# Layer 2 of a two-layer recurrent trunk: keys and values turned by VectorE and through DRAM instead of by TensorE, Silu as one function, and another plan

## The chip, the cores and the metric

The kernel runs on one core of a Trainium2 chip. Its engines are TensorE (PE), VectorE (DVE), ScalarE (ACT), GpSimd (POOL) and SyncE (SP, which here only issues DMAs). The metric is the device time of one launch in microseconds, as the median of several runs.

## The reference

One step of a decoder trunk with two layers, over 1024 new prompt positions and 8 sampled sequences of 4 positions, 1056 tokens in all, with 1024 features. Layer 1 is an RG-LRU block. Layer 2, which the change is about, is an HGRN2 block with eight heads of 128 key and 128 value features:

```python
u = (rmsnorm(x) @ w_in)                    # 1024 -> 4 * 1024: q, f, iv, gate
q = silu(q)
log_g = logaddexp(log(lb), log1p(-lb) + log_sigmoid(f));  k = -expm1(log_g);  v = iv
# per head, a recurrence over time, computed in chunks:
#   S_t = exp(log_g_t) * S_(t-1) + k_t v_t^T ;  o_t = q_t S_t
o = o * rsqrt(mean(o * o) + EPS) * o_gain
x = x + (o * silu(gate)) @ w_out
```

Outputs are the final normed activations and the states of both layers.

## The kernel before, in words

Everything is stored with features on the 128 partitions and the 1056 tokens along the free dimension. Large products are made in three parts (`mm3`, L243 to L245): both operands are split into a high and a low part, and high times high, high times low and low times high are added in PSUM. The splits of weights are made by ACT (the high part, L380 and L1430) and POOL or DVE (the low part, L325).

**Order.** Each layer is written as a list of operations with costs, keys read and written, and priorities (class `Flow`). A planner on the host simulates the engines with these costs, turns the plan forward and back eight times, and issues all instructions in the order of the best plan. PE's operations marked `main` are chained, so their order is fixed by the program text. Layer 1 also runs a random search of 3000 tries over its first 60 us; layer 2 does not.

**Layer 2.** Heads 0 and 1 are projected with plain products (`item`, evacuation from L1001), heads 2 to 7 by `seven`: a scheme with seven half-size products in place of eight, called twice per head, first for queries and forget gates (`seven(h, 0, 1, ...)`), then for gates and values (`seven(h, 3, 2, ...)`). Four weight loads per call go out on SP (L1423). The finished quarters are settled in `settle`: forget gates by Tanh (L1511) and two affine steps (L1512, L1513), queries and gates by a hand-made Silu, `0.5 x (1 + tanh(0.5 x))` without its half: Tanh on ACT (L1517), then (t + 1) * x on DVE (L1518; in `item` L1018, in layer 1's `first1` L717). The missing halves are made good later: `4 * EPS` at L1299 and `hog`, half the output gain, at L1327.

**The recurrence.** Per head it is cut in chunks of 128 tokens, and within a chunk in levels 1, 2, 4 to 64: at each level DVE scales queries (row A) or keys (row B) by decays (`scale`, L1036, with ACT copying the other half, L1039), and PE makes small blocks of scores in column tiles (`diag`, L1054, and L1074, L1088, L1108, L1132, L1139). Four bursts per head are put between the big products. In their order:

- `burst1(h)`: levels 0 and 1 of head h. Of head h-1 the keys (both halves) and the second half of the values are turned by `transposed`: four PE transposes per half (L1163) into PSUM and an ACT copy to SBUF (L1169). The sampled tokens are turned apart (`samples`, L1175).
- `burst2(h)`: levels 2 and 4 of head h; of head h-1 the state products, `kt` times `vt` for each chunk (`states`, L1219, eight of 128 x 128 x 128), the sampled states (L1227) and their update (`advance`, L1248).
- `burst3(h)`: levels 8 and 16 of head h; outputs of head h-1 (`outs`, L1273 with the values, L1275 with the states), then Square sums on ACT (L1292) and the normalisation.
- `burst4(h)`: levels 32 and 64 of head h, and the first half of its values is turned; outputs of head h-1 are turned back and multiplied with the gate (`gated`, L1317, L1327).

The first two stand in the second call of `seven` for head h, the last two in the first call for head h+1.

So the keys of head h are final after `scale(h, 64, 0, 0)` in `burst4(h)` and are used in `burst2(h+1)`; the values are read there and in `burst3(h+1)`. Between `burst4(h)` and `burst2(h+1)` lie about eight pairs of big products. The turned keys `kt` share their buffer with the outputs `on`.

**After the heads** comes the output projection, whose first products (with the first five heads) cover the bursts of head 7, and the final norm.

Of the kernel before, what the change touches and what calls it, by code (L numbers as in the profile page):

```python
# [41 lines left out]
CH = 352  # L42
# [9 lines left out]
class Flow:  # L52
# [3 lines left out]
    HOP = 0.2  # L56
    ENGINES = ("PE", "DVE", "ACT", "POOL", "SP")
# [37 lines left out]
    def lag(self, i, j):  # L95
# [4 lines left out]
        return self.HOP + b[6] + (2.15 + a[5] / 250.0 if a[5] else 0.0)  # L100

    def plan(self, key, stop=None):
# [5 lines left out]
        free = dict.fromkeys(self.ENGINES, 0.0)  # L108
        dma = 0.0
# [4 lines left out]
        for _ in range(n):  # L114
# [6 lines left out]
            if both and free["POOL"] > t0:  # L121
                us = max(us, free["POOL"] - t0 + us - 0.13)
            starts[i] = t0
            free[e] = end = t0 + us
            if kb:
                dma = max(dma, t0 + 2.6) + kb / 250.0
                end = dma - 2.15 - kb / 250.0
            ends[i] = max(free[e], dma if kb else 0.0)
# [83 lines left out]
def tile_trunk(ctx: ExitStack, tc: tile.TileContext, xT, prm, hc, w0, wg, wo0, w1, wo1, s_in,  # L212
# [85 lines left out]
    with ExitStack() as l0:  # L298
# [15 lines left out]
        def act(n, emit, r, w, prio=5, more=0.0):  # L314
            fl.add("ACT", 0.25 + 0.0007 * n + more, emit, r, w, prio)

        def dve(n, emit, r, w, prio=5, both=False):
            fl.add("DVE", 0.13 + 0.0011 * n, emit, r, w, prio, both=both)

        def pool(n, emit, r, w, prio=5):  # L320
            fl.add("POOL", 0.1 + 0.00245 * n, emit, r, w, prio)
# [69 lines left out]
        def product(w, xs, step=8, more=()):  # L391
# [3 lines left out]
            for s in range(0, n, step):  # L395
# [6 lines left out]
                fl.add("PE", 0.48 * len(ks), emit, (*(q for k in ks for q in (*xs[k][2], *w(k)[2])), *more), (pk,), 1, main=True)  # L402
# [305 lines left out]
        def first1(i, c):  # L708
# [64 lines left out]
        def smalls1():  # L773
# [6 lines left out]
            nonlocal lc, lcn, lbc, hog  # L780
            mx, e0, e1, lb, lc, lcn, lbc, hog = (small(8) for _ in range(8))
# [14 lines left out]
            v(V.tensor_scalar, hog, pv("og"), 0.5, None, op0=ALU.mult)  # L796
# [41 lines left out]
        hbr = hbi = hbd = cn = cp = lc = lcn = lbc = hog = None  # L838
# [90 lines left out]
    with ExitStack() as l1:  # L929
        p1 = l1.enter_context(tc.tile_pool(name="l1", bufs=1, reuse_waits="tile"))  # L930
        fl = Flow(side=0.4)
# [21 lines left out]
        kt = fixed("kt", [128, 8, 128], F32, p1)  # L953
        on = kt
# [3 lines left out]
        vt = rows[5][:, :1024].rearrange("p (n d) -> p n d", n=8)  # L958
        SA = a_rows[1]
        for o, n, keys in ((at, 1024, ATK), (ad, 256, [("ad",)]), (as2, 64, [("as", 0), ("as", 1)]),  # L960
                           (ab, 288, [("ab",)])):
            pool(0.3 * n, lambda o=o: G.memset(o, 0.0), (), keys, 3)
# [852 lines left out]
```

## Time and profile before

| what | value |
|---|---|
| runs | 1060.86, 1060.86, 1060.49 us; median 1060.86 |
| profiled execution | span 1059.4 us from its first to its last instruction |
| between the span and the median of the runs | 1.5 us |
| instructions in the profile | 25677 |
| granted PE clock over the span | 0.996 |
| bytes moved by DMA | 103.07 MB, on average 97 GB/s |

The profile is that of one execution; the time of that execution itself, other than by its span, is not recorded, so its span is set beside the median. In its rows a number after L is a line of the kernel. PE lists its matmuls, PEld its weight loads. A float32 product leaves two matmul records, a transpose one. Durations of matmuls overlap, so neighbouring rows of the timeline are compared by their starts.

### The profile page before, as it was taken

The numbers are of one execution on the slowest core, as the hardware profiler recorded it, in microseconds if no ns is written. First come the engines' busy times: TensorE is split into PE (matmuls) and PEld (weight loads), VectorE is DVE, ScalarE is ACT, GpSimd is POOL, SyncE is SP. The second block draws the span as 40 slices with busy tenths as digits, with TensorE's granted clock in tenths as the row PEclk, the third lists the DMA queues.
The fourth block names the chain that finished last, engine by engine and source line by source line (L and its number), as shares of the span: only waits on it lengthen the run. The fifth ranks groups of instructions, "written<-read, shape, count | busy, mean of one in ns | idle before, by whom it ended". The sixth has DMA issues, their size and how long they took to land.

```text
span 1059.4 us, 25677 instructions
## 1 busy us (share of the span) xinstructions
PE 1050.1 (99%) x9964; PEld 1021.2 (96%) x9964; DVE 842.2 (79%) x1671; ACT 590.9 (56%) x1339; POOL 540.0 (51%) x601
## 2 busy tenths in 40 slices
PE   9999999999999999999999999999999999999997
PEld 9999999999999999999999999999999999999986
DVE  7999996888888689265799988988979797994536
ACT  6568656877775875233354474646464555652324
POOL 3425343444544366555667555555545565551544
PEclk9999999999999999999999999999999999999998
DMA  8201112123842595340211121212121221355204
GB/s 297 68 27 45 54 51 74 57 60 100 255 145 63 177 294 162 127 136 28 71 44 38 45 101 44 92 45 92 35 91 54 72 70 66 117 177 167 84 3 164
DMA packets 70121, 103.07 MB, mean 97 GB/s; under 512 B 9200, under 2 KB 50160, under 8 KB 70000
## 3 DMA queue, kind: packets, MB, share of 16 engines
q1 hardware_dynamic: 67696, 98.67, 29.2%
q10 hardware_dynamic: 2304, 2.77, 0.8%
q8 instruction: 78, 1.28, 0.5%
q14 instruction: 43, 0.35, 0.1%
HBM read 71.05 MB, written 25.49 MB: 91 GB/s over the span
## 4 chain that ended last, share of the span: by engine, by line
PE 89%; DVE 6%; DMA 2%; POOL 1%; issue 1%; ACT 0%; ACTq 0%; POOLq 0%; DVEq 0%; SPq 0%
PE mm L243 24%; PE mm L244 24%; PE mm L245 24%; PE hg L569 1%; PE hg L1054 1%; PE hg L1163 1%; DVE R L1370 1%; PE hg L1273 1%; DMA wraw<-in_w_dram 1%; PE hg L1219 1%; PE hg L243 1%; PE hg L244 1%; PE hg L245 1%; PE hg L1275 1%; DVE tmp L1370 1%
## 5 line engine op out<-in xcount | busy, mean ns | idle before, releaser
L243 PE MATMUL mm<-xh,whi 128*128 128x352 f32 (+1 forms) x1143 | 358.6, 314 | 0.0
L245 PE MATMUL mm<-xh,wlo 128*128 128x352 f32 (+1 forms) x1143 | 353.2, 309 | 0.0
L244 PE MATMUL mm<-xl,whi 128*128 128x352 f32 (+1 forms) x1143 | 353.1, 309 | 0.0
L325 POOL TENSOR_TENSOR wlo<-wraw,whi 128x256 fp32r<-128x256 f32 (+3 forms) x184 | 203.3, 1122 | 178.6 <-ACT whi L380 81.2
L244 PEld LDWEIGHTS mm<-xl,whi 128*128 128x128 f32 x1143 | 215.1, 188 | 1.5
L243 PEld LDWEIGHTS mm<-xh,whi 128*128 128x128 f32 x1143 | 214.7, 188 | 1.5
L245 PEld LDWEIGHTS mm<-xh,wlo 128*128 128x128 f32 x1143 | 214.8, 188 | 0.0
L501 DVE SCALAR_TENSOR_TENSOR k<-xb,prm_sb,k 128x352 f32<-128x352 f32 (+2 forms) x144 | 90.1, 637 | 10.9 <-ACT k L498 7.7
L243 PE MATMUL mm<-t,whi 128*128 128x264 f32 (+1 forms) x306 | 89.3, 292 | 0.0
L244 PE MATMUL mm<-t,whi 128*128 128x264 f32 (+1 forms) x306 | 87.7, 287 | 0.0
L245 PE MATMUL mm<-t,wlo 128*128 128x264 f32 (+1 forms) x306 | 87.4, 286 | 0.0
L1503 DVE TENSOR_TENSOR k<-mm,k 128x264 f32<-128x264 f32 x144 | 60.2, 426 | 20.5 <-PE mm L245 17.4
L325 POOL TENSOR_TENSOR wlo<-R,whi 128x256 fp32r<-128x256 f32 x64 | 60.1, 959 | 24.7 <-ACT whi L1430 24.7
L584 POOL TENSOR_TENSOR k<-X 128x352 f32<-128x352 f32 x36 | 44.9, 1257 | 47.8 <-DVE R L585 38.6
L380 ACT CAST whi<-wraw 128x512 fp32r<-128x512 f32 (+2 forms) x83 | 46.1, 574 | 30.1 <-PE mm L244 16.1
L243 PEld LDWEIGHTS mm<-t,whi 128*128 128x128 f32 x306 | 57.6, 188 | 0.2
L245 PEld LDWEIGHTS mm<-t,wlo 128*128 128x128 f32 x306 | 57.7, 188 | 0.0
L244 PEld LDWEIGHTS mm<-t,whi 128*128 128x128 f32 x306 | 57.6, 188 | 0.0
L1430 ACT CAST whi<-wraw 128x512 fp32r<-128x512 f32 x52 | 32.1, 618 | 36.3 <-PE mm L245 16.8
L243 PE MATMUL mm<-yh,whi 128*128 128x352 f32 x153 | 49.9, 326 | 0.0
L245 PE MATMUL mm<-yh,wlo 128*128 128x352 f32 x153 | 49.4, 323 | 0.0
L244 PE MATMUL mm<-yl,whi 128*128 128x352 f32 x153 | 49.4, 323 | 0.0
(481 smaller groups left out, 2634.3 us busy)
## 6 DMA issues: line engine op xcount, KB each, us to landing
wraw<-in_w_dram SPq DMA_DIRECT2D x90, 256.0 KB, 2.7
wraw<-in_wo_dram SPq DMA_DIRECT2D x34, 192.0 KB, 2.5
si<-in_s_in_dram SPq DMA_DIRECT2D x8, 512.0 KB, 3.8
out_ss_out_dram<-si SPq DMA_DIRECT2D x8, 512.0 KB, 2.6
R<-in_w_dram SPq DMA_DIRECT2D x15, 256.0 KB, 2.5
sg<-x1b SPq DMA_DIRECT2D x21, 176.0 KB, 2.9
x<-sg SPq DMA_DIRECT2D x21, 176.0 KB, 1.8
R<-td SPq DMA_DIRECT2D x72, 44.0 KB, 2.0
```

Of the source, the lines that this page charges most:

```text
L243: T.matmul(out, wh, xh, start=first, stop=False)
L244: T.matmul(out, wh, xl, start=False, stop=False)
L245: T.matmul(out, wl, xh, start=False, stop=last)
L325: emit = lambda: e.tensor_tensor(b, x, a.bitcast(F32), op=ALU.subtract)
L380: act(m, lambda hi=hi, raw=raw, m=m: S.copy(hi[:, :m], raw[:, :m]), rk, (hk,), prio)
L501: dve(u, lambda src=src, dst=dst, sh=sh, k=k: V.scalar_tensor_tensor(dst, sh(src, k), pc("cw", 12 * k + m), dst, op0=ALU.mult, op1=ALU.add ...
L569: fl.add("PE", 0.62, lambda ps=ps, i=i, c=c: T.matmul(ps[:96, :CH], gs[:, i, :], ST[:96, chunk(c)], start=True, stop=True), (("gs",), *((" ...
L584: pool(CH, lambda x=x, a=a, b=b: G.tensor_tensor(x, a.bitcast(F32), b.bitcast(F32), op=ALU.add), (ak, bk), (xk,), 3)
L1054: T.matmul(ps[32 * j:32 * j + 32, n * w:n * w + w], B[:, o:o + 32], q(slice(o, o + 32)), start=True, stop=True, tile_position=(0, 32 * j))
L1370: dve(n, lambda: V.tensor_tensor(o, a, b, op=op), r, (w,), prio, True)
L1430: act(512, lambda: S.copy(hi, raw), (rk,), (hk,), 2)
L1503: dve(QT, lambda: V.tensor_tensor(o[0], z[0], u[0], op=ALU.add), (z[1], u[1]), (o[1],), 0)
```

## The change

The change has three parts, all in layer 2 except for two lines of `first1`.

1. `transposed` goes. At the end of `burst4`, `turned` turns values and keys of the head: DVE transposes blocks of 32 x 32 over 1024 columns, the result is written to DRAM (512 KB) and read back in four parts of 128 KB, so that the 32-token blocks of each chunk land on their partitions. Afterwards the features of a row lie in four blocks of 32, 256 columns apart. A state product therefore becomes four, with 32 weight columns each, in four column tiles of PE; the values are read as a moving operand with four pieces.
2. Queries and gates get Silu on ACT in one step, straight from PSUM or the sums; the DVE step goes, and so do the factors that made up for the half.
3. The planner has its own costs for layer 2 (`exact`), starts from the time at which each engine ends layer 1, keeps SP's and ACT's DMA queues apart, and lets DVE operations marked `both` and POOL operations exclude each other. The search over the first 60 us is made for layer 2 too. The weight loads of `seven` go out on ACT's queue instead of SP's.

```diff
 class Flow:
+    HOPS = {"PE": 0.23, "DVE": 0.15, "ACT": 0.15, "POOL": 0.15, "SP": 0.2}
-    def __init__(self, until=None, side=1.2):
+    def __init__(self, until=None, side=1.2, busy=None):
+        self.busy = {e: (busy or {}).get(e, 0.0) for e in self.ENGINES}
+        self.exact = busy is not None
...
     def plan(self, key, stop=None):
-        free = dict.fromkeys(self.ENGINES, 0.0)
-        dma = 0.0
+        free = dict(self.busy)
+        locked = taken = 0.0
+        dma = {"SP": 0.0, "ACT": 0.0}
...
-            if both and free["POOL"] > t0:
+            if both and not self.exact and free["POOL"] > t0:
                 us = max(us, free["POOL"] - t0 + us - 0.13)
+            elif both and self.exact:
+                us += max(0.0, taken - t0 - 0.07)
+                locked = t0 + us
+            elif e == "POOL" and self.exact:
+                us += max(0.0, locked - t0 - 0.035)
+                taken = t0 + us
...
         def act(n, emit, r, w, prio=5, more=0.0):
-            fl.add("ACT", 0.25 + 0.0007 * n + more, emit, r, w, prio)
+            fl.add("ACT", (0.09 + 0.00088 * n if fl.exact else 0.25 + 0.0007 * n) + more, emit, r, w, prio)
...
         def first1(i, c):
-                act(CH, lambda: S.activation(o, ps[:, :CH], AF.Tanh, scale=0.5), (pk,), ok, 0)
-                dve(CH, lambda: V.scalar_tensor_tensor(o, o, 1.0, ps[:, :CH], op0=ALU.add, op1=ALU.mult), (pk, *ok), ok, 0)
+                act(CH, lambda: S.activation(o, ps[:, :CH], AF.Silu), (pk,), ok, 0)
...
-        fl = Flow(side=0.4)
+        last = {e: max(t[3] for t in fl.log if t[1] == e) for e in Flow.ENGINES}
+        fl = Flow(side=0.4, busy={e: max(0.0, t - last["PE"]) for e, t in last.items()})
...
-        vt = rows[5][:, :1024].rearrange("p (n d) -> p n d", n=8)
+        vflat = rows[5][:, :1024]
+        vt, kt = (o.rearrange("p (a n j) -> p n a j", a=4, n=8) for o in (vflat, kflat))
+        VK, KK = ([(o, i) for i in range(4)] for o in ("vt", "kt"))
+        turn = {(o, i): nc.dram_tensor(f"{o}_{i}", (128, 1024), F32, kind="Internal").ap() for o in ("vt", "kt") for i in range(2)}
...
-        def transposed(row, rk, dst, key, parts):
...
-                        T.transpose(ps[:, n * 128:(n + 1) * 128], row[:, a:a + 128], ident)
...
-                act(512, lambda i=i, ps=ps: S.copy(dst[:, 4 * i:4 * i + 4, :].rearrange("p n d -> p (n d)"), ps), (pk,), ((key, i),), 2)
+        def turned(h, row, rk, dst, key, keys):
+
+            d = turn[key, h % 2]
+            dve(1024, lambda: V.transpose(dst, row[:, :1024].rearrange("p (n b i) -> p b n i", n=8, b=4)), rk, keys, 3, True)
+            dma(d, dst, keys, ((key, "d", h % 2),), 3, 512)
+            back = d.rearrange("(a i) (b m) -> b i a m", a=4, b=4)
+            for b in range(4):
+                dma(dst[32 * b:32 * b + 32].rearrange("p (a m) -> p a m", a=4), back[b], ((key, "d", h % 2),), (keys[b],), 3, 128)
...
         def states(h, s, sk):
-                        T.matmul(ps[:, n * 128:(n + 1) * 128], kt[:, 4 * i + n, :], vt[:, 4 * i + n, :], start=True, stop=True)
-                pe(0.94, emit, (("kt", i), ("vt", i)), (pk,))
+                        for a in range(4):
+                            w = slice(32 * a, 32 * a + 32)
+                            T.matmul(ps[w, n * 128:(n + 1) * 128], kt[:, 4 * i + n, a], vt[:, 4 * i + n], start=True, stop=True,
+                                     tile_position=(0, 32 * a))
+                pe(1.05, emit, (*KK, *VK), (pk,))
...
         def burst1(h):
-            run(together([*([levels01(h, *s)] if h < H else []), *([keys_(h - 1, *s), values(h - 1, (1,), *s)] if h else [])]))
+            run(together([*([levels01(h, *s)] if h < H else []), *([keys_(h - 1, *s), values(h - 1, *s)] if h else [])]))
...
         def burst4(h):
-            run(together([*([gated(h - 1, *s)] if h else []), *([levels3264(h, *s), values(h, (0,))] if h < H else [])]))
+            run(together([*([gated(h - 1, *s)] if h else []), *([levels3264(h, *s)] if h < H else [])]))
+            if h < H:
+                turned(h, VT, [("VT", c) for c in range(4)], vflat, "vt", VK)
+                turned(h, *brow(h, 0), kflat, "kt", KK)
...
         def seven(h, a, b, order, at=()):
-                dma(t, src, (), (k,), 2, 256)
+                dma(t, src, (), (k,), 2, 256, S)
...
         def settle(h, i, a, c, ck):
-                act(QT, lambda: S.activation(o[:, q], c, AF.Tanh, scale=0.5), (ck,), k, 0)
-                dve(QT, lambda: V.scalar_tensor_tensor(o[:, q], o[:, q], 1.0, c, op0=ALU.add, op1=ALU.mult), (ck, *k), k, 0, own)
+                act(QT, lambda: S.activation(o[:, q], c, AF.Silu), (ck,), k, 0)
...
         with tc.manual_schedule(engines={E.PE, E.DVE, E.Activation, E.Pool, E.SP}):
-            fl.run()
+            fl.run(SEARCH, 60.0)
```

The other lines give operations of layer 2 new planned costs (for instance 0.95 in place of 1.1 for levels 0 and 1) and change keys and names to fit.

More of the change, by code (lines that the diff above doesn't have):

```diff
@@ L1200, in keys_ @@
         def keys_(h, s, sk):
-            B, bk = brow(h, 0)
-            yield from together([transposed(B, bk, kt, "kt", (0, 1)), samples(krep, "krep", s, sk, 64, kst, "kst", 1)])
+            yield from samples(krep, "krep", s, sk, 64, kst, "kst", 1)
         def together(gens):
@@ L1651, in tile_trunk @@
         spare = []
[L1652 removed]
+        for o, olds in ((R[:, 0], eight("A", 1)), (SA, [("SA", i) for i in range(2)]), (rows[5], VK),
                         (SG[6], ykeys(0, 0, TOK))):
```

98 lines of the change are left out of this document (42 added, 56 removed).

## Prediction

> **What bounds the kernel now.** First the page: the busy shares and the chain of work that ended last.
>
> ```profile
> PE 1050.1 (99%) x9964; PEld 1021.2 (96%) x9964; DVE 842.2 (79%) x1671; ACT 590.9 (56%) x1339; POOL 540.0 (51%) x601
> ...
> PE 89%; DVE 6%; DMA 2%; POOL 1%; issue 1%; ACT 0%; ACTq 0%; POOLq 0%; DVEq 0%; SPq 0%
> ```
>
> TensorE (PE) has work 99% of the time and is 89% of the chain. The share is an average, so the next view is the busy time by stretches: the start of layer 2, all that follows up to the end of PE's work, and one head of it.
>
> ```profile
> core 0: us, PE busy (x) PEld busy (x) DVE busy (x) ACT busy (x) POOL busy (x), PEclk, DMA share, GB/s
> 508.00:568.00 60.00, 59.03 (x766) 57.25 (x765) 54.71 (x96) 26.12 (x62) 43.04 (x39) 1.00 0.17 55
> 604.00:1046.00 442.00, 442.00 (x5638) 424.44 (x5637) 347.36 (x756) 225.88 (x601) 234.31 (x266) 1.00 0.25 83
> 660.20:716.90 56.70, 56.70 (x806) 54.82 (x806) 47.60 (x104) 30.63 (x80) 31.60 (x38) 1.00 0.21 71
> ```
>
> From 604 to 1046 us PE is never without work, at the full granted clock (1.00). A head takes 56.7 us, and in it VectorE (DVE) is busy 47.6, ScalarE (ACT) 30.6, GpSimd (POOL) 31.6. So in this stage an instruction taken from PE shortens the program by its whole issue interval, and work on DVE or ACT costs nothing while it is in time. Only the start of layer 2 is different: there DVE has 54.7 of 60 us, and the view of waits (us in total, times, longest) has PE waiting for it twice.
>
> ```profile
> PE hg L1108 <- DVE a L1036: 0.5, 1, 0.5
> PE hg L1054 <- DVE R L1066: 0.4, 1, 0.4
> ```
>
> These are 0.9 us in all, so a better plan of layer 2 has about that much to win. A matmul's duration overlaps the next one, so what an instruction costs PE is the step from its start to the next start. Here is PE in one head: the two places that turn keys and values (L1163), and the state products (L1219).
>
> ```profile
> 672.78 0.66 PE L1163 MATMUL hg<-ident,sg 128*128 128x128 f32 x4
> 673.20 0.37 PE L243 MATMUL mm<-t,whi 128*128 128x264 f32 x1
> ...
> 688.02 1.10 PE L1054 MATMUL hg<-R,a 128*32 128x64 f32 x64
> 688.94 0.28 PE L1074 MATMUL hg<-R,a 128*32 128x64 f32 x2
> 689.15 0.66 PE L1163 MATMUL mm<-ident,sg 128*128 128x128 f32 x4
> 689.64 0.60 PE L1163 MATMUL hg<-ident,sg 128*128 128x128 f32 x4
> 690.08 0.38 PE L1175 MATMUL hg<-ident,krep 128*96 128x128 f32 x2
> 690.29 0.60 PE L1163 MATMUL hg<-ident,sg 128*128 128x128 f32 x4
> 690.73 0.38 PE L1175 MATMUL hg<-ident,vrep 128*96 128x128 f32 x2
> ...
> 699.78 0.73 PE L1054 MATMUL hg<-R,a 128*32 128x32 f32 x62
> ...
> 701.07 1.16 PE L1219 MATMUL mm<-sg,kt 128*128 128x128 f32 x8
> ...
> 703.05 0.64 PE L1227 MATMUL hg<-si,ab 128*32 128x128 f32 x16
> 703.63 0.50 PE L1248 MATMUL hg<-vb,kst 96*128 96x512 f32 x1
> ```
>
> **The change part by part.** *Transposes leave PE.* A run of four takes 0.42 us (672.78 to 673.20), 0.49, 0.44 and 0.44: 1.79 per head. The first of a run starts slowly (0.49 against 0.44), which the next instruction inherits, so I count 0.44 / 4 = 0.11 us each. The busy time of L1163 alone, in all of layer 2, gives the count.
>
> ```profile
> 508.00:1046.00 538.00, 18.72 (x128) 14.02 (x128) 1.00 0.24 78
> ```
>
> 128 x 0.11 = **14.1 us** off PE (bounds 13.5 to 14.3), all of it on the path except perhaps some of head 0's 1.8 us, which falls where DVE is the tight one.
>
> *State products are cut in four.* The turned keys lie in blocks, so each 128-wide product becomes four with 32 weight columns in four column tiles, 32 per head in place of 8 (each leaves two records). Now they take 703.05 - 701.07 = 1.98 us. The nearest row is L1227, with the same 32 columns and 128 moving elements: 8 products in 0.58 us, so 32 take 2.32, +0.34 per head. But its 0.58 holds the entry to and the exit from one short run. From the other side, L1054 issues 64 records with 32 moving elements in about 0.57 us (62 of them from 699.78, with 0.55 to the next line) and with 64 in 0.92 (688.02 to 688.94); on that line 128 would take 0.92 + 2 x 0.35 = 1.62, -0.36 per head. I take 2.05, a little nearer to L1227: +0.07 per head, **+0.5 us** for eight heads, with the ends -2.9 and +2.7. The products with the values as moving operand (L1273) keep their count; only their step through memory changes, and L1054's two-piece operand shows no extra for that.
>
> *DVE.* It loses the second half of the hand-made Silu (L1018, L1518) and gets two block transposes of 1024 elements per head. The first row is L1518's busy time over the six heads of `seven`, the second the nearest row to a transpose.
>
> ```profile
> 604.00:944.00 340.00, 27.26 (x48) 1.00 0.24 79
> ```
>
> ```profile
> L1066 DVE TENSOR_TENSOR R<-R,ST 128x1056 f32<-128x1056 f32 x6 | 9.7, 1610 | 0.3
> ```
>
> Eight per head at 27.26 / 48 = 0.57 us are 4.5 us less. No row shows a transpose. L1066, two inputs over 1056 elements, takes 1.61; one input in blocks could be half of that or, element for element, twice: 0.8 to 3.2 each. I take L1066's 1.6, so DVE goes to 47.6 - 4.5 + 3.2 = 46.3 us per head, and at the dear end 49.5, of a new period of 55. Either way PE covers it. [...]
>
> *ACT.* Four PSUM evictions of 0.59 us go; one Silu takes the place of one Tanh. New on its queue are eight weight loads per head (from SP).
>
> ```profile
> L1169 ACT COPY sg<-hg 128x512 f32<-128x512 f32 x10 | 5.9, 589 | 0.2 <-PE hg L1163 0.2
> ```
> ```profile
> 681.32 4.60 SPq L312 DMA_DIRECT2D wraw<-in_w_dram  x3
> 687.63 0.33 SPq L312 DMA_DIRECT2D R<-in_w_dram  x1
> ```
>
> On SP such loads wait for their buffer: three took 4.60 us to get out, where the next, alone, took 0.33. On ACT whatever stands behind waits too: the weight casts L1430 and the settling of results. ACT is idle 26 of 56.7 us, and by the code casts are made four products ahead of PE (NW = 4), so I take nothing; without that cover it is up to a few us per head (below).
>
> *The way through DRAM.* Turned keys and values go out (512 KB) and come back in four parts of 128 KB in 1 KB pieces.
>
> ```profile
> si<-in_s_in_dram SPq DMA_DIRECT2D x8, 512.0 KB, 3.8
> out_ss_out_dram<-si SPq DMA_DIRECT2D x8, 512.0 KB, 2.6
> ```
> ```profile
> 678.64 0.69 DVE L1036 TENSOR_TENSOR sg<-sg 128x512 f32<-128x512 f32 x1
> ```
>
> Write 2.6, four issues 1.3, the reads 3.8 as 512 KB in one: 7.7 us, and for the second of the pair on SP some 4 more, as it waits for the first write and its issues. Keys are final at 679.3 (the end of L1036's step for level 64), and are used at 701.07: 21.8 us for two turns (3.2) and some 12 us of transfers. Six to seven are left; at the dear end of the turns (6.4) three, and reads at twice 3.8 would use these up, so this cover is the thinnest. SP's other DMAs queue behind the ten new ones per head, state loads, state stores and gated rows, none of which is due within 10 us; the weight loads, which were, have left SP.
>
> *The plan.* That VectorE and GpSimd exclude each other is a rule in the host's plan; on the chip it changes only the order of instructions. PE's main order is fixed by the chain of its operations, so I count nothing: between -0.9 (both waits above gone, DVE being lighter there too) and new waits, below. The head of layer 1's plan is made by the same search over slightly other operations; I take nothing, plus or minus 1.
>
> **Sum.** The span is 1059.4 us and the median of the runs 1060.86, so 1.5 lies around it. 1059.4 - 14.1 + 0.5 = 1045.8; with 1.5, **1047.3 us**.
>
> **Rivals.** *A, as reckoned*, 1044.5 to 1049.5.
>
> *B, column tiles are cheap*: L1054's line holds and both waits go: 14.1 + 2.9 + 0.9 off, 1043.0.
>
> *C, a new wait takes a part back*: weight loads on ACT hold up a cast, or the transposes come between DVE results that PE needs soon. For: DVE is busy 84% of a head and POOL shares its time; ACT now waits for buffers. Against: ACT and DVE together have less to do. At 0.6 us per head over eight heads: 1052.1.
>
> *D, the gain is used up*: the exchange does nothing in sum, because DVE after all sets the pace; that needs 55 - (47.6 - 4.5) = 12 us for two transposes. 1060.9.
>
> *E, slower*: ACT has to reload its function table between Silu and Tanh. The place is the settling of each head.
>
> ```profile
> L588 ACT ACT_TABLE_LOAD x12 | 15.4, 1283 | 0.2
> ```
> ```profile
> 672.32 0.42 ACT L1511 ACTIVATE a<-k 128x264 f32<-128x264 f32 x1 [0.85 <-PE hg L1132]
> ...
> 678.03 0.41 ACT L1511 ACTIVATE a<-k 128x264 f32<-128x264 f32 x1
> ```
>
> The forget gates (L1511, stays Tanh) stand together, four from 672.32 to 678.03, and queries and gates (L1517, become Silu) before and after them: two switches per head, 16 in all, 16 x 1.28 = 20.5 us. If each reaches PE in full, 1067.8; it is slower from two thirds of that (13.6 of 20.5). For: layer 1 shows twelve such loads before its square roots (L588). Against: Tanh, Square, Identity and Copy alternate through layer 2 without one load, and ACT's idle 26 us per head can take 2.6. [...]
>
> **How the numbers follow.** A 0.62, B 0.06, C 0.18, D 0.04, E 0.10 (with it any other path to slower, such as keys that come late). A measurement of this kernel can tell about 0.2%, 2.1 us, from no change. Faster: A, B and C, 0.86; same: D, 0.04; slower: E, 0.10. The range from 1043 to 1054 holds A, nearly all of B and some three quarters of C, 0.8; it takes in both ends of the state products and 0.5 us of new waits per head.
>
> **What would show it.** No L1163 on PE, and a head period of about 55.0 us in place of 56.7. The state products 1.6 to 2.3 us per head. Transposes on DVE with their first duration, 0.8 to 3.2. One table load at layer 2's first Silu; two per head would be E. PE still without idle between 604 us and the end; an idle row released by DMA before the state products would mean that keys came late, one released by ACT casts would be C. I am wrong if the head's period isn't shorter, or if PE waits more than 1 us per head.

## The result, and the profile after

The changed kernel takes 1062.78 us (median of 12 runs, 1060.35 to 1064.98) beside 1060.73 for the kernel before (12 runs, 1060.08 to 1061.26): a ratio of 1.0019, with a 95% interval of 1.0011 to 1.0028. The prediction was 1047.3. So the time did not fall by 13 us; it rose by 2, about the limit of what this measurement can tell. The changed kernel's runs spread over 4.6 us where those of before spread over 1.2, and its six longest have the lower mean granted clock (0.992 to 0.994, against 0.995 to 0.997 in the six shortest), so the loss of clock described below differs from run to run, and the profiled execution is one of the longer. The profiled execution of the changed kernel took 1063.88 us, with a span of 1062.2 us (before: 1059.4).

The page has the expected first row: TensorE (PE) is busy 8.4 us less than before, VectorE (DVE) 13.4, ScalarE (ACT) 17.4, GpSimd (POOL) 23.4.

```profile
PE 1041.7 (98%) x10220; PEld 1011.9 (95%) x10220; DVE 828.8 (78%) x1626; ACT 573.5 (54%) x1308; POOL 516.6 (49%) x601
...
PE 90%; DVE 4%; DMA 3%; POOL 1%; issue 1%; ACT 0%; ACTq 0%; POOLq 0%; SPq 0%; DVEq 0%
```

Less work and more time: PE must now wait, or work more slowly. Busy time by stretches shows where. The rows are one head without a wait, one head with one, 15 us around head 2's second burst, the start of layer 2, and the long stretch in which PE never waited before.

```profile
core 0: us, PE busy (x) PEld busy (x) DVE busy (x) ACT busy (x) POOL busy (x), PEclk, DMA share, GB/s
...
777.49:832.43 54.94, 54.88 (x840) 53.07 (x839) 45.35 (x98) 27.95 (x75) 28.03 (x37) 1.00 0.36 109
665.15:721.48 56.33, 55.12 (x839) 53.05 (x838) 47.39 (x106) 28.14 (x75) 28.95 (x37) 1.00 0.39 111
645.00:660.00 15.00, 11.35 (x252) 10.66 (x251) 11.47 (x25) 3.83 (x10) 7.56 (x12) 0.77 0.32 76
508.00:568.00 60.00, 58.44 (x701) 57.16 (x700) 46.66 (x79) 24.32 (x58) 40.03 (x41) 1.00 0.29 89
604.00:1046.00 442.00, 434.92 (x5876) 416.46 (x5875) 340.84 (x730) 210.56 (x576) 218.41 (x267) 0.99 0.39 117
```

The first row is the predicted head: 54.94 us in place of 56.70, with 55.0 forecast. But from 604 to 1046 us PE is idle for 7.1 us where it never was before; the head from 665 has 1.2 of them, and in the 15 us from 645 PE lacks 3.65 us and has only 0.77 of its clock. The view of waits names them (us in total, times, longest).

```profile
PE hg L1222 <- DVE R L1447: 3.6, 1, 3.6
PE hg L1222 <- issue: 2.1, 2, 1.1
PE hg L1069 <- ACT R L1054: 1.6, 1, 1.6
...
PE hg L1231 <- issue: 0.9, 1, 0.9
PE mm L1231 <- issue: 0.7, 1, 0.7
```

L1222 are the state products (L1219 before), L1231 the sampled ones. They wait once for 3.6 us, and four times in all for "issue", that is, for nothing that the profile shows. The first row names a VectorE operation, but that one doesn't concern the state products; by the code they wait for the keys read back from DRAM, and by the trace the last of these lands at 650.86 us, 0.35 us before the state products start. The rows of the trip stand below.

Where a head is undisturbed, the parts of the change did what was forecast or better. The timeline of PE at the two places where work was taken away or changed:

```profile
696.77 1.10 PE L1069 MATMUL hg<-R,a 128*32 128x64 f32 x64
...
697.89 0.46 PE L1182 MATMUL hg<-ident,krep 128*96 128x128 f32 x2
698.19 0.38 PE L1182 MATMUL hg<-ident,vrep 128*96 128x128 f32 x2
698.33 0.37 PE L254 MATMUL mm<-t,whi 128*128 128x264 f32 x1
```
```profile
820.97 1.95 PE L1222 MATMUL hg<-sg,kt 128*32 128x128 f32 x64
822.72 0.65 PE L1231 MATMUL mm<-si,ab 128*32 128x128 f32 x16
823.29 0.50 PE L1252 MATMUL hg<-vb,kst 96*128 96x512 f32 x1
```

The burst that held three runs of transposes is 1.56 us long, and the state products step from 820.97 to 822.72, 1.75 us in place of 1.98, although they are four times as many. The block transposes, which no row of before could show, take 1.24 us each:

```profile
L1172 DVE STREAM_TRANSPOSE sg<-sg 128x1024 f32<-128x1024 f32 x8 | 10.0, 1244 | 2.1 <-PE hg L1277 0.9 <-ACT sg L1019 0.8 <-PE hg L1279 0.4
L1172 DVE STREAM_TRANSPOSE kt<-sg 128x1024 f32<-128x1024 f32 x8 | 9.9, 1240 | 0.1
```

**The four losses.** In the profiled executions, comparing the starts of the same bursts in the two traces:

- *Layer 1.* The first burst of layer 2 starts at 524.82 us instead of 521.13: 3.7 us lost before the change proper begins.
- *Start of layer 2.* PE waits 1.76 us between two products at 538.33 (1.6 in the view of waits, for ACT's half of a scaling, L1054). Before, it waited at L1108, one burst later, for 0.5, and there it now doesn't wait; together about 1.1 us are lost.
- *Head 1's keys.* The second burst of head 2 lasts 10.05 us, about 6 more than the 4.0 of undisturbed heads: the wait, and then products at a granted clock of 0.5.
- *"Issue" breaks* of 1.15, 1.37, 0.95 and 1.31 us inside the second bursts of four of the seven heads that have state products in them: 4.8 us.

Together nearly 16 us; the heads gain 13 to 14. The rest of this document is about these losses.

### The profile page after: what moved, and what is told of

It is laid out like the page before. It is cut to its first block, busy times and chain, and to the rows that moved or that the text cites. A ratio compares the mean times of both kernels' runs of the same rounds, so it can differ in the third digit from the quotient of the medians.

```text
span 1062.2 us, 26195 instructions
## 1 busy us (share of the span) xinstructions
PE 1041.7 (98%) x10220; PEld 1011.9 (95%) x10220; DVE 828.8 (78%) x1626; ACT 573.5 (54%) x1308; POOL 516.6 (49%) x601
## 3 DMA queue, kind: packets, MB, share of 16 engines
q8 instruction: 80, 1.31, 0.5%
## 4 chain that ended last, share of the span: by engine, by line
PE 90%; DVE 4%; DMA 3%; POOL 1%; issue 1%; ACT 0%; ACTq 0%; POOLq 0%; SPq 0%; DVEq 0%
PE mm L254 25%; PE mm L255 25%; PE mm L256 25%; PE hg L1069 1%; PE hg L1222 1%; PE hg L581 1%; PE hg L1277 1%; PE hg L1279 1%; PE hg L254 1%; PE hg L256 1%; PE hg L255 1%; DMA wraw<-in_w_dram 1%; DMA R<-in_xT_dram 1%; PE hg L1252 1%; PE mm L1069 1%
## 5 line engine op out<-in xcount | busy, mean ns | idle before, releaser
L337 POOL TENSOR_TENSOR wlo<-wraw,whi 128x256 fp32r<-128x256 f32 (+3 forms) x184 | 192.2, 1060 | 213.2 <-ACT whi L392 101.8
L1510 DVE TENSOR_TENSOR k<-mm,k 128x264 f32<-128x264 f32 x144 | 60.1, 425 | 25.8 <-PE mm L256 24.8
L337 POOL TENSOR_TENSOR wlo<-R,whi 128x256 fp32r<-128x256 f32 x64 | 56.8, 906 | 35.6 <-ACT whi L1437 26.4
```

What stands on the lines that cost most here:

```text
L337: emit = lambda: e.tensor_tensor(b, x, a.bitcast(F32), op=ALU.subtract)
L1510: dve(QT, lambda: V.tensor_tensor(o[0], z[0], u[0], op=ALU.add), (z[1], u[1]), (o[1],), 0)
```

## The experiments

Each run is compared with the kernel before on the same chip, in 1060.7 to 1061.2 us.

**Layer 1 as before.** The lines of `first1` and the half gain are put back:

```diff
-                act(CH, lambda: S.activation(o, ps[:, :CH], AF.Silu), (pk,), ok, 0)
+                act(CH, lambda: S.activation(o, ps[:, :CH], AF.Tanh, scale=0.5), (pk,), ok, 0)
+                dve(CH, lambda: V.scalar_tensor_tensor(o, o, 1.0, ps[:, :CH], op0=ALU.add, op1=ALU.mult), (pk, *ok), ok, 0)
```

> The changed kernel with layer 1's operations as they were (Tanh and the DVE step in first1, the half gain computed and unused), so that layer 1's plan is the old one; head 0's queries are then doubled, and its EPS is four times larger to match. Theory (the gain on PE is there and is given back in four places, the first of them layer 1, whose plan comes out otherwise): layer 1 ends 3.6 us earlier, as before, 1059.2 us in place of 1062.8. Rival (PE's slightly longer step in layer 1, 160.8 against 159.9 ns, belongs to the execution and not to the plan): under 1 us of it goes, 1062.

Measured: 1057.52 us (ratio 0.9965, 0.9951 to 0.9979), 5.3 below the changed kernel. Two lines that aren't meant for speed, in a layer that the change is not about, cost more than the whole result. The first burst is back at 520.79 us, and the wait for head 1's keys is 2.6 instead of 3.6 us.

**The turns planned earlier.** The planner counts 4 us more for each DMA of the turned rows, out and back, so that it places them earlier:

```diff
-        return (self.HOPS[a[0]] if self.exact else self.HOP) + b[6] + ...
+        return (self.HOPS[a[0]] if self.exact else self.HOP) + (4.0 if a[4] == 3.01 else 0.0) + b[6] + ...
-            dma(d, dst, keys, ((key, "d", h % 2),), 3, 512)
+            dma(d, dst, keys, ((key, "d", h % 2),), 3.01, 512)
...
```

> The changed kernel, with 4 us more planned for each transfer of turned keys and values, so that the plan puts the turns sooner. Theory (the keys of head 1 reach the state products 3.8 us late, and PE then runs some us at half clock): both go, 6.0 us less, 1056.8 us, and no wait over 1 us before the state products except those that the profile calls issue. Rival (the transfers are slow because they meet the weight loads, wherever they are put): the wait stays above 2 us, 1061 or more.

Measured: 1061.1 us (1.0003, 0.9994 to 1.0013). The wait is gone and PE keeps its clock (1.00 from 645 to 660 us, where the changed kernel had 0.77), some 6 us, but the time falls by 1.7 only. The view of waits of this run has what took its place:

```profile
PE mm L255 <- DVE xl L337: 2.0, 3, 1.0
PE mm L254 <- DVE k L1510: 1.2, 3, 0.6
```

At 623 to 632 us the big products now wait for DVE, which makes the low halves of `seven`'s operands (L337) and adds up its results (L1510) there. From the start of one burst there, at 616.93 us, to the start of the next, at 638.56, PE takes 21.63 us, with DVE busy for 20.63, where the changed kernel takes 17.65 (618.05 to 635.70): the 4 us are lost there. So by this plan DVE is the tight engine around head 1, and two transposes placed early push out something else. That another order has room for them, the run with the old rules shows below.

**State products in four, in the kernel before.** Nothing but the split; the transposes stay on PE:

```diff
-                        T.matmul(ps[:, n * 128:(n + 1) * 128], kt[:, 4 * i + n, :], vt[:, 4 * i + n, :], start=True, stop=True)
+                        for a in range(4):
+                            w = slice(32 * a, 32 * a + 32)
+                            T.matmul(ps[w, n * 128:(n + 1) * 128], kt[:, 4 * i + n, w], vt[:, 4 * i + n, :], start=True, stop=True,
+                                     tile_position=(0, 32 * a))
```

> The kernel before, with each state product cut in four column tiles of 32, and nothing else changed. Theory (96 short records more per head let PE run out of instructions: waits of about 1.2 us called issue in about half of the heads): the products themselves take 1.72 in place of 1.98 us, 2.1 less, the waits cost 4.7, together 1063.5 us. Rival (those waits belong to the turned data or its transfers): no such wait, 1058.8 us. A second rival (column tiles are as dear as the nearest row, 2.3 us per head): 1063.5 without waits over 0.5 us.

Measured: 1064.3 us (1.0031, 1.0018 to 1.0044), 3.6 above the kernel before. The products themselves are cheaper here too: an undisturbed burst takes 3.81 us instead of 4.18, and the last, with the state products of head 7 alone, 2.65 instead of 2.79: 7 x 0.37 + 0.14 = 2.7 us off. But five breaks appear, 6.5 us: 6.5 - 2.7 = 3.8, near the 3.6 measured. The first row of its waits:

```profile
PE hg L1221 <- issue: 4.4, 4, 1.4
```

**Layer 2 by the old rules of the plan.** `fl = Flow(side=0.4)` and `fl.run()` as before, all else as changed.

> The changed kernel with the old rules for layer 2's plan: old costs, no exclusion of DVE and POOL, one DMA queue, no search. Theory (the new rules are worth about 1 us at layer 2's start and nothing after it, as PE's order is fixed): 1062 to 1065 us. Rival (the new rules themselves put the turns late, and so cost the wait for keys): the wait goes, 1057 us. Another (the new rules are what keeps DVE and POOL apart and PE supplied): waits in most heads, over 1070 us.

Measured: 1057.06 us (0.9964, 0.9951 to 0.9977), 5.7 below the changed kernel. Head 1's keys come in time: its values are turned at 623.19 us and its keys at 629.77, against 630.55 and 634.66, and the burst takes 4.08 us; PE has no idle time in the stretch before it (618.61 to 635.58). The breaks stay (1.16, 2.12, 0.97, 1.43 us).

**Where the breaks are.** Up to here five kernels had breaks, and they have one thing in common that no view shows at once. If PE's instructions (a weight load and a product each) are numbered as the trace lists them, every break stands at number 193 or 194 modulo 256. I call the 256 numbers from one such place to the next a block, and the place its border. The page of the changed kernel has a queue of instructions whose counts go with PE's:

```profile
q8 instruction: 80, 1.31, 0.5%
```

80 packets, 1.31 MB, 16 KB each; PE has 20,577 instructions in the trace, 257 per packet (the kernel before has 20,037 and 78 packets, again 257). A packet starts at 586.07, 708.22, 765.66 and 876.02 us, and each break ends 2.4 to 2.8 us after that (at 588.90, 710.69, 768.02, 878.68). So the theory, an estimate from these counts and times: there is one packet to a block, and where PE gets to a border sooner than some 2.4 to 2.8 us after the packet's start, it stands still until then. No view shows what is in a packet. Among the big products, at 122 to 161 ns per record, with two instructions each, a block lasts 16 to 21 us, and no break stands among them. A second burst has 130 records of scores at some 10 ns, then 64 of state products at 27 and 16 of sampled ones at 36: 420 instructions in 4 us. In the four breaks the packet started 0.7 to 1.5 us after PE had begun the block ahead, in the dense stretch. How fast a block is used up doesn't decide by itself: PE went through one in 1.38 us from 819.60 without a break, as the next packet had started 1.6 us ahead of that. In the kernel before a second burst had 324 (the states are 16 records, not 64), and there is no break at all. This timeline is one break (708 to 711 us of the changed kernel):

```profile
708.73 0.86 PE L1222 MATMUL hg<-sg,kt 128*32 128x128 f32 x24
710.69 1.30 PE L1222 MATMUL hg<-sg,kt 128*32 128x128 f32 x40 [1.10 <-issue]
```

**An unused tile.** Layer 1's loss had a second side. Over the same 400 us of layer 1 with PE never idle, PE issues fewer products:

```profile
100.00:500.00 400.00, 400.00 (x2467) 1.00 0.38 118
```
```profile
100.00:500.00 400.00, 400.00 (x2453) 1.00 0.39 118
```

The first row is of the kernel before, the second of the changed one, both at the full granted clock. The 352-column products of layer 1 step in 160.28 ns before and in 160.99 after (means of the middle four fifths). To ask whether it is where the operands lie, one more small tile was taken:

```diff
-            mx, e0, e1, lb, lc, lcn, lbc = (small(8) for _ in range(7))
+            mx, e0, e1, lb, lc, lcn, lbc, _ = (small(8) for _ in range(8))
```

> The changed kernel with one more small tile of 8 values per partition in layer 1 that nothing uses, in the place where the removed half gain stood; every engine's list of instructions is the same as in the changed kernel, only the addresses of the tiles behind it are those of the kernel before. Theory of the layout: the products of 352 columns step in 160.99 ns in the changed kernel and in 160.28 ns in the kernel before because their rows lie elsewhere; here they step in 160.3 again, 2,650 of them in layer 1 give 1.9 us back and some 670 in layer 2 another 0.5, so the first burst of layer 2 starts near 522.9 instead of 524.8 and the time is near 1060.4. Theory of the plan: the pace comes from what ScalarE and VectorE do beside the products in the new order, the step stays at 160.99, and the time stays at 1062.8 within 0.5.

Measured: 1062.93 us (1.0016, 1.0006 to 1.0025), the step 160.99 ns. The experiment missed, and says nothing on the theory: the small tiles are pieces of one fixed tile, and no row of an operand moved. By the code, the addresses of rows are given in the order of their first use, so they follow the plan of layer 1; the addresses of the input halves and weight pieces differ between the two kernels, and every run up to here had the slow step (160.99 ns in the changed kernel and here) with the one set of addresses and the fast step (160.28 in the kernel before) with the other.

**Both undone.** Layer 1 as before and layer 2 by the old rules.

> The changed kernel with layer 1 as it was (Tanh and a VectorE product, half gain kept) and with layer 2 planned by the rules of before. If the two losses are separate, the 5.3 and 5.7 us that they gave one by one add up but for the 0.9 us that both took from the wait for the keys of head 1: 1062.8 - 5.3 - 5.7 + 0.9 = 1052.7. The rival: both repair the same thing (where layer 2 begins against its transfers), then little is added, 1056 to 1057. The waits of TensorE named issue should remain in four of the eight heads, some 5 to 6 us in sum, under either.

Measured: 1052.65 us (0.9924, 0.9907 to 0.9940). The two losses are separate: 5.3 and 5.7, less the 0.9 us that both took from the wait for head 1's keys, are the 10.1 measured.

**Half a block.** The same with 32 more products (128 instructions) in the first burst of layer 2:

```diff
-            pe(0.95, lambda: diag(ps, B, lambda q: av[:, :, q], 64), r, (pk,))
+
+            def emit():
+                for _ in range(32 if h == 0 else 0):
+                    T.matmul(ps[:32, :32], B[:, :32], av[:, 0, :32], start=True, stop=True)
+                diag(ps, B, lambda q: av[:, :, q], 64)
+
+            pe(0.95, emit, r, (pk,))
```

> The run that undoes both, with 32 small products more at the head of layer 2's first burst, whose result is overwritten: 128 instructions of TensorE, half a block of 256. Theory of the instruction supply: every stall of TensorE inside a burst so far begins at the same place of its stream, instruction 193 or 194 modulo 256 of the trace, so the stalls move: the second bursts of heads 1, 3, 4 and 6, which had them (1.2, 2.1, 1.0 and 1.4 us with the rules of before), and the others swap in part; expected are stalls near the instructions 273 of head 1's burst, 333 of head 2's, none or little in head 3's, 291 in head 4's, 399 in head 5's, none in head 6's, 359 in head 7's, about 6 us in sum, and the time within 2 us of the run it is made from, with the 0.6 us that the 32 products take. Rival: the stalls come from what the other engines and the queues do at those times; then heads 1, 3, 4 and 6 keep theirs, at the same products.

Measured: 1055.28 us (0.9947, 0.9933 to 0.9962). The breaks move as forecast. Length in us, in brackets the instruction of the burst at which the break stands, counted from the trace:

```
second burst of head        1           2           3           4           5           6           7
state products of head      0           1           2           3           4           5           6
changed kernel              1.15 (401)  keys late   1.37 (311)  0.95 (417)  -           1.31 (373)  -
both undone                 1.00 (400)  -           1.37 (310)  1.05 (418)  -           1.10 (378)  -
both undone, half a block   -           1.34 (333)  -           0.77 (290)  0.53 (398)  -           1.54 (358)
before, states in four      1.63 (368)  1.07 (398)  -           1.62 (298)  1.56 (376)  -           0.65 (275)
```

The bursts of heads 1, 3 and 6 lost theirs, those of heads 2, 5 and 7 got one, and each that came is within one instruction of an expected place. Here is the burst of head 2 with both undone, first, and with half a block more:

```profile
643.48 1.96 PE L1223 MATMUL hg<-sg,kt 128*32 128x128 f32 x64
```
```profile
645.29 1.25 PE L1229 MATMUL hg<-sg,kt 128*32 128x128 f32 x35
647.62 0.96 PE L1229 MATMUL hg<-sg,kt 128*32 128x128 f32 x27 [1.07 <-issue]
```

Nothing else in layer 2 was changed, so in these runs the breaks go by PE's own count and not by what the other engines do. One expected break missed: at instruction 273 of head 1's burst PE went on, and the sum is 4.2 us in place of about 6. The time is 2.6 us longer, not the 0.6 expected: by the second burst of head 1 the run is 1.5 behind, for the 32 products and what they delay; the breaks are about as long in sum (4.2, and 4.5 in the run that it is made from).

**States apart.** The same as "both undone", with the state products in a burst of their own, one big product later. The core of it:

```diff
-FQ0, FQ, GV = "126b74b35", "12b675b43", "126b754b3"
+FQ0, FQ, GV = "126b74b35", "12b675b43", "126b754b3b"
...
+        def burst2b(h, s):
+            run(together([states(h - 1, *s), advance(h - 1, 0)]))
...
```

> The run that undoes both, with the state products and the first advance put into a burst of their own, one product (24 steps of TensorE, about 3 us) after the scores of the same burst, so that no burst has more than some 260 short instructions in a row. Theory of the instruction supply: the stalls of 5 to 6 us in sum go, the time is about 1052.7 - 5.5 + 0.5 for seven more changes between long and short products = 1047.7. Rival, stalls from other engines' doings: they stay wherever the state products stand, 1052 to 1053.

Measured: 1047.89 us (0.9879, 0.9864 to 0.9893). In this kernel the sample queries of the next head are copied ahead of the products that still read the last head's, so the sampled outputs are made from the wrong head's queries; the amount of work is the same. No break is left. The next run has the copy in its right place:

```diff
         def burst2b(h, s):
             run(together([states(h - 1, *s), advance(h - 1, 0)]))
+            samples_q(h)
...
```

> The run with the state products in a burst of their own, with the copy of the sample queries put behind the products that read the former head's (in the earlier run it stood ahead of them, and the sample outputs were of the wrong head's queries). Nothing else differs, no stall is expected in a burst: 1047.9 within 0.7, 13 us under the kernel before, which is what the prediction reckoned for the transposes alone (14.1 less 0.5). Rival: the copy, on GpSimd, comes late for the head after; then a wait of TensorE shows at the sample products and the time is 1049 to 1051.

Measured: 1048.2 us (0.9879, 0.9865 to 0.9894). The head's row and PE's longest waits:

```profile
653.40:708.40 55.00, 55.00 (x840) 53.10 (x839) 46.52 (x99) 28.14 (x75) 28.77 (x37) 1.00 0.35 109
```
```profile
PE hg L742 <- DVE ones L266: 1.0, 1, 1.0
PE hg L1070 <- DVE R L1082: 0.9, 1, 0.9
PE mm L254 <- DVE sg L541: 0.9, 1, 0.9
```

A head of 55.00 us without idle time, and no row released by "issue". The span is 1045.5 us, where the prediction's sum was 1045.8.

**Rows placed as before.** The changed kernel, instruction for instruction in its own order, with the input halves, weight pieces and long rows cut out of larger tiles, so that they lie at the addresses of the kernel before:

```diff
+        o = acts.tile([128, 16 * TOK], F32R, tag="P", bufs=1, name="x")
+        return [[o[:, i * TOK:(i + 1) * TOK] for i in p] for p in ((0, 15, 12, 9, 8, 5, 11, 4), (14, 13, 10, 7, 6, 3, 1, 2))]
...
```

> The run with the unused small tile did not move the rows, so it tested nothing: the rows of the operands are placed in the order of their first use, and that follows the plan of layer 1. This run is the changed kernel with every row that layer 1's products read (high and low halves of the input, weight pieces) and the nine long rows at the addresses of the kernel before, and with all its instructions in the order of the changed kernel. Theory of the addresses: the step of the 352-column products goes by where the operands lie; 3,640 undisturbed steps of 161.06 ns become 160.08 ns again, 3.6 us, of which some 2.7 by the first burst of layer 2 (near 522.1 instead of 524.8), and the time is 1062.8 - 3.6 = 1059.2. Rival, the order of layer 1's work beside the products: the step stays at 161 and the time at 1062.8.

Measured: 1058.83 us (10 runs, 1056.13 to 1060.61; 0.9981, 0.9971 to 0.9990), 4.0 below the changed kernel. The step is 160.31 ns, the first burst of layer 2 starts at 521.85 us, and layer 1 has its old count:

```profile
100.00:500.00 400.00, 400.00 (x2467) 1.00 0.40 118
```

So of layer 1's 3.7 us, 3.0 are the addresses, and 0.7 the plan. (This trace is of the shortest of the ten runs; the 4.0 us are between medians. The undisturbed steps alone, some 3,640 over both layers, go from 161.07 to 160.13 ns on the mean, which is worth 3.4 us.)

**New rules, states apart.** As the run with the states apart, but with the new rules in layer 2.

> As the run before, but layer 2 planned by the rules of the changed kernel. With layer 1 as it was, the new rules cost 1057.5 - 1052.7 = 4.9 us, and the second burst of head 1's successor lasted 9.16 us against 4.14. Theory: all of that is the late keys; the state products, now about 3 us after the scores, wait 0 to 1 us for them, TensorE doesn't fall to half its clock, and the time is 1048 to 1049.5. Rival: the rules cost by what else they place; then 1051.5 to 1053.

Measured: 1047.73 us (0.9876, 0.9861 to 0.9891), the same as by the old rules. The new rules cost nothing once the state products come about 3 us later; their 5.7 us in the changed kernel came by way of head 1's late keys and the clock of 0.5 after them. One break is left, of 0.7 us at 641.0, at number 193.

**Silu in both layers.** As the run with the states apart and the old rules, with layer 1 as changed and its rows placed as before.

> As the run with the states apart, but layer 1 as the changed kernel has it (Silu, no VectorE product) with its rows at the addresses of before. Theory: Silu in layer 1 costs nothing of itself, and what the changed kernel lost there was the addresses and about 1 us in the first 45 us by the plan: 1048 to 1049. Rival: the plan of layer 1 with Silu is itself worse by the 3.7 us that it lost: 1051.5.

Measured: 1049.3 us (0.9890, 0.9875 to 0.9905): 1.1 more than with Tanh in layer 1, of which 0.8 stand at the first burst already (521.93 against 521.14). Silu in layer 1 is no gain, and hardly a loss.

Counted over all fourteen traces, between 555 and 1000 us, there are 44 breaks of over 0.45 us inside bursts. 40 begin at number 193 or 194 modulo 256; the other four are the waits for head 1's keys. Of the four versions with the states apart, three have none.

The count also says where the breaks came. In no trace does PE get past the border of a block sooner than 2.2 us after the start of its packet, and the 40 breaks end 2.2 to 2.9 us after it. Counted as in the table, every border that fell on instruction 275 of a burst or later had a break: there are 37, of 0.4 to 2.1 us. Those that fell earlier, up to 273, had none of more than 0.2 us, with one exception: near instruction 206 of head 2's second burst four of eleven traces break, by 0.5 to 1.1 us (the 0.7 us of the run with the new rules and the states apart is one of them). There the packet starts 1.7 to 2.6 us after PE has begun the block ahead, and in the other seven at most 1.5; why is not shown. With the states apart a burst has at most some 260 instructions, so it doesn't reach 275. In the kernel before, no border falls beyond instruction 248 of a second burst, so its having no break doesn't show that 324 are safe.

## Why the prediction was wrong, point by point

*Transposes leave PE, 14.1 us*: right. The two bursts that lost them are 1.28 and 0.42 us shorter per head (1.56 for 2.84, 2.14 for 2.56), 1.70 of the 1.79 counted, or 13.6 over eight heads. With the losses removed, the span is 13.9 us shorter than before, where the sum had 13.6. That these two meet so closely is partly luck: the transposes gave a little less than counted and the state products a little more, and the run has layer 1 and the plan's rules as before.

*State products, +0.07 us per head*: wrong in sign, inside the bounds. They step in 1.75 us, 0.23 less (an undisturbed burst as a whole takes 4.0 to 4.1 us in place of 4.18). L1054's line (1.62) was the nearer figure, not the short run of L1227. But the bounds left out the breaks: the step failed in counting only the time of the 32 short products, and not that a second burst goes from 324 instructions to 420. The breaks cost 4.8 us in the changed kernel. The row "issue 1%" of the chain and the row of the instruction queue were on the page of before; nothing there could have shown such a cost, since in before no border fell beyond instruction 248 of a second burst, and there was no break.

*DVE, two transposes at 1.6*: 1.24 each, and 45.35 us in an undisturbed head (46.52 in the one of the run with the states apart) against 46.3 reckoned.

*ACT, nothing*: right for the weight loads; no row of PE's waits is released by a cast. The one wait released by ACT (1.6 us, L1054) is of a scaling at the start of layer 2. Rival E did not come: the trace has no table load at the settling of queries and gates (L1524), where sixteen were feared.

*The way through DRAM*: the sizes were right (some 12 us), the place was wrong. I took the slack from head 2, 21.8 us, and called it the thinnest cover. Head 1 is thinner, and before's trace says so: level 64 ends there at 628.9 and the state products start at 644.3.

```profile
628.18 0.69 DVE L1036 TENSOR_TENSOR sg<-sg 128x512 f32<-128x512 f32 x1
```
```profile
644.34 2.05 PE L1219 MATMUL hg<-sg,kt 128*128 128x128 f32 x16
```

15.4 us for 3.2 of turns and 12 of transfers leave 0.2. In the changed kernel the chain reads, on DVE, SP's queue and PE:

```profile
629.94 0.69 DVE L1051 TENSOR_TENSOR sg<-sg 128x512 f32<-128x512 f32 x1
...
634.66 1.23 DVE L1172 STREAM_TRANSPOSE kt<-sg 128x1024 f32<-128x1024 f32 x1
```
```profile
637.36 0.32 SPq L323 DMA_DIRECT2D kt<-kt  x1
...
643.26 2.33 SPq L323 DMA_DIRECT2D kt<-kt  x4
```
```profile
646.81 0.75 PE L1069 MATMUL hg<-R,sg 128*32 128x32 f32 x64
651.21 3.64 PE L1222 MATMUL hg<-sg,kt 128*32 128x128 f32 x64 [3.65 <-DVE R L1447]
654.60 1.11 PE L1231 MATMUL mm<-si,ab 128*32 128x128 f32 x16
655.64 0.79 PE L1252 MATMUL hg<-vb,kst 96*128 96x512 f32 x1
```

The scaled rows are ready at 630.6, the turn of the values and other DVE work hold the turn of the keys back by 4 us, the write leaves at 637.4 and lands 5.8 us later, and the reads, the first of them issued when it has landed, take 5.7 to 6.5 us. Their groups on the page:

```profile
kt<-kt SPq DMA_DIRECT2D x8, 512.0 KB, 3.4
kt<-kt SPq DMA_DIRECT2D x32, 128.0 KB, 6.1
```

The prediction named keys that come late, as one of "any other path to slower" in rival E's tenth, and gave it no price. And the wait has a second half that no step reckoned: after it PE has a granted clock of 0.5, and 64 records take 3.39 us from start to start instead of 1.75. The granted clock of the trace is 0.5 from 649.64 to 656.47 us, 6.83 us; in the run with layer 1 as before it is 0.5 for 3.41 us (0.89 on the mean from 645 to 660 us). In the changed kernel it fell 2.1 us after PE's last record had ended (647.56), in a wait of 3.65 us in all; in the run with layer 1 as before the whole wait was 2.6 us. A wait of 1.9 us in the trace with the rows placed as before left the clock at 1.00. What decides when the clock falls, and for how long, these three waits do not show.

*The plan, nothing*, and *layer 1, plus or minus 1*: these, both put at nothing, are the steps that failed most. Taking the new rules away gave 5.7 us, taking layer 1's change away 5.3. The first loss comes by way of head 1's keys, for with the state products later the new rules cost nothing. The second has a cause that the prediction did not have in view: the plan of layer 1 also decides where its rows lie, and that is worth 4.0 us of time (1062.78 against 1058.83 with the rows placed as before).

*The chances*: 0.86 for faster rested on each loss being small by itself. They were four, from four sides, and added up to more than the gain. Rival C had the form of it (a new wait takes a part back) at under a third of the size.

What stays open: what in the addresses makes the step longer. The step is the same to 0.1 ns in the runs with the same addresses (160.99 ns in the changed kernel and with the unused tile, 160.28 and 160.31 in the kernel before and with the rows placed as before), but the traces hold no addresses, and no run was made on it. Open too is why the packet comes late in head 2's burst in some plans.

## What to carry to other kernels

When a step is moved, look for the head or the round in which it has the least slack, not a typical one: here the first round after a change of scheme had 0.2 us where the steady ones had 6. When many short instructions take the place of a few long ones, count the instructions in a row, and try a few long ones between two dense stretches: here seven second bursts of up to 420 instructions had four breaks and the late keys, and with some 260 in a row at most, and about 3 us of big products before the rest, three of four versions had no break. And when a host plan orders the work, an edit anywhere can move operands and waits everywhere: run the edit with its parts undone one by one before believing that a part is worth nothing.

The version with the transposes off PE, layer 1 as it was and the state products a product later beats both kernels: 1047.7 to 1048.2 us, 1.2% under the kernel before.

## What the hardware showed beside that

- The queue of instructions shows packets of 16 KB, 80 in the changed kernel for 20,577 instructions of PE and 78 in the kernel before for 20,037, 257 per packet. Numbered as the traces list them, 40 of 44 breaks begin at number 193 or 194 modulo 256, and in no trace does PE pass such a border sooner than 2.2 us after the start of its packet. Where the border fell on instruction 275 or later of a burst of records of 10 to 36 ns, PE stood still for 0.4 to 2.1 us (37 of 37).
- The same f32 products, 352 columns wide, step in 161.07 ns in the changed kernel and in 160.13 with the rows placed as before (means over layers 1 and 2, the instructions in the same order), at a granted clock of 1.00 from 100 to 500 us in both; 0.6%, some 3.4 us in this kernel.
- A block transpose of 128 x 1024 f32 on DVE took 1.24 us (1244 and 1240 ns, means of eight each); a TENSOR_TENSOR over 1056 elements took 1.61 (mean of six, in the kernel before).
- The reads of 128 KB took 6.1 us (median) for the keys and 3.4 for the values; the keys' reads go out beside a state load of 512 KB, whose median is 6.4 us here and was 3.8 before, and in most heads beside weight loads from ACT's queue too. No run separates these.
